# A two-layer transformer on one Trainium2 core: TensorE's order in the expert loop fixed and staggered over three pairs, bank copies on ScalarE

## The chip, the core and the metric

The kernel runs on one core of one Trainium2 chip, in one launch. The time is device microseconds of a whole execution, the lower the better. Three executions of the kernel before took 1410.09, 1410.16 and 1411.47 us; the median is 1410.16 us.

## The reference

The model has two layers over 512 tokens of width 1024, in float32. Layer 0 mixes tokens with differential attention, layer 1 with a compressed, selected and windowed attention; each layer then adds a mixture of 32 experts, of which every token uses two:

```python
pg = softmax(t @ w_grp + b_grp);  p_top, grp = top_k(pg, 1)         # 4 groups of 8 experts
le = einsum('td,gde->tge', t, w_exp) + b_exp                        # router inside a group
val, idx = top_k(le[arange(T), grp[:, 0]], 2)
wts = softmax(val) * p_top
...
a = silu(einsum('td,edh->teh', t, w_gate)) * einsum('td,edh->teh', t, w_up)   # 1024 -> 256, per expert
y = y + einsum('teh,ehd->td', a * combine, w_down)                            # 256 -> 1024
x = x + g2 * y
```

The expert weights of one layer are 32 x 3 MB; all of them pass through the core once per layer.

## The kernel before, in words

After the router, every expert has a list of up to 64 tokens. Two experts make a **pair**: 64 rows of the one and 64 rows of the other fill the 128 partitions. There are 16 pairs a layer, and per pair (function `pair`) these steps:

- **gather** (line 838, a DMA that GpSimd's queue issues): the 128 token rows go to the tile `xg`, which has two buffers.
- **rows** (line 852): 8 transposes of 128x128 on TensorE, four to each of two PSUM banks `tr`; 8 copies out of the banks that apply scale and shift (lines 857 and 859, by turns ScalarE and VectorE) make `xT`.
- **gate-up** (line 864): 16 calls, 8 pieces of the width for each of two experts. Each uses half of the array's columns (64 stationary columns; the output goes to partitions 0 to 63 or 64 to 127), and the two experts' calls run side by side. A call is two MATMUL records in the trace. Then SiLU `sl` on ScalarE (line 867) and the product `ac` on VectorE (line 869).
- **by hidden** (line 873): 2 transposes of `ac` into a `tr` bank and a copy out, `aTm` (lines 394 and 395, by turns ScalarE and VectorE).
- **down** (line 887): 8 calls, again on half of the columns each; then `y` (line 890, VectorE), and its split into two reduced-precision parts, `yh` (line 370, ScalarE) and `yl` (line 371, VectorE).
- **add** (lines 898 and 899): a 0/1 matrix `st` (line 881) scatters the pair's rows back to the tokens: 8 outputs of 128x512 (4 token tiles x 2 halves of the width), each the sum of two matmuls on the full array; VectorE adds each to the residual `xs` (line 900).

Steps on the full 128 stationary columns (rows, by hidden, add) are called **full-tile work** below, gate-up and down **half-column work**. PSUM has 8 banks of 512 floats a partition: four tagged `mm`, two `tr`, two `sc`. A bank is given again when its readers are done. The gate-up's bank and the second half of every down and add are `mm`, the first half of every down and add `sc`.

In the loop of `experts` the add of pair q-1 is called inside pair q, behind its by-hidden transposes. That is the order of the program's text only: the scheduler of the framework orders each engine's instructions itself by a simulated timeline, TensorE's too, so a pair's adds and transposes may be woven into gate-up and down. What an engine does is fixed when the program is built.

Weights come from one queue, that of SyncE (SP, line 114), in pieces of 512 KB. Gate and up of five experts and down of six are in SBUF at a time (`N_GU`, `N_DN`); a piece waits until the matmuls that read its place last are done, and until the piece eight places ahead of it has landed (`DEPTH_X`). Ahead of the loop, `overflow` holds a second copy of the pair's code for experts with more than 64 tokens, behind a branch; with these inputs it isn't entered.

## Time and profile before

| | |
|---|---|
| median of 3 executions | 1410.16 us |
| the profiled execution | 1411.33 us, of which the profile's span 1409.5 us |
| mean granted TensorE clock | 0.956 of full speed |
| TensorE busy | 1282.6 us (91%) |
| VectorE, ScalarE, GpSimd busy | 786.7 us (56%), 514.6 us (37%), 169.4 us (12%) |
| DMA | 309.8 MB, mean 220 GB/s |
| gate-up matmuls (line 864) | 1024 MATMUL records |
| copies out of the `tr` banks (lines 857, 859) | 128 on ScalarE, 128 on VectorE |

The two expert loops lie at about 397 to 679 us (layer 0) and 1117 to 1399 us (layer 1) of the span. The profile's slices show TensorE nearly always busy in them; since matmuls are pipelined and their ends are modelled, that says little, and the loop is better read by the time from pair to pair.

### The profile page before, as it was taken

Reading aid. Unit: us, or ns where it says so; the run is one execution under the profiler, and the core shown is the slowest. Engines: PE = TensorE matmul, PEld = TensorE weight load, DVE = VectorE, ACT = ScalarE, POOL = GpSimd, SP = SyncE. Lnnn points to the kernel's source line nnn. Section 1 sums busy time; section 2 is a strip of 40 time slices with the busy share of each in tenths; the row PEclk is TensorE's granted clock in tenths of the full one; section 3 lists DMA queues with packets and bytes.
Section 4 is the critical chain, followed back from the end, with each engine's and each line's share of the span. In section 5 each row is a group of like instructions: output and inputs, shape, how many; then the busy total and the mean of one; then the engine's idle time right before and its main releaser. Section 6 shows DMA issues by size and latency. Waiting matters only on the chain. (4 is left out here: it accounts for less than half of the span.)

```text
span 1409.5 us, 18225 instructions
## 1 busy us (share of the span) xinstructions
PE 1282.6 (91%) x6431; PEld 759.2 (54%) x6431; DVE 786.7 (56%) x1791; ACT 514.6 (37%) x1188; POOL 169.4 (12%) x298
## 2 busy tenths in 40 slices
PE   4899999978879999999799799999999699999995
PEld 0687668567733544444588555555568434444342
DVE  2454755485635666655554365656635446666555
ACT  2454544454322222111454444656644212222212
POOL 0021020211110000000042111111220200000000
PEclk7899999999989999999899899999999699999998
DMA  7633764585579999992332174510153599999931
GB/s 253 219 104 112 244 209 150 180 289 193 185 244 363 390 405 408 379 350 95 109 120 90 60 255 147 148 51 1 54 161 120 182 362 369 407 408 409 364 141 60
DMA packets 104493, 309.81 MB, mean 220 GB/s; under 512 B 13776, under 2 KB 27568, under 8 KB 104388
## 3 DMA queue, kind: packets, MB, share of 16 engines
q1 hardware_dynamic: 93920, 288.59, 57.4%
q0 software_dynamic: 6240, 12.95, 2.7%
q10 hardware_dynamic: 4228, 6.96, 1.6%
q8 instruction: 55, 0.90, 0.3%
q14 instruction: 50, 0.41, 0.1%
HBM read 310.51 MB, written 6.33 MB: 225 GB/s over the span
## 5 line engine op out<-in xcount | busy, mean ns | idle before, releaser
L864 PE MATMUL b_mm<-slot,xT 128*64 128x512 f32 x640 | 199.3, 604 | 0.0
L864 PE MATMUL b_mm<-ring,xT 128*64 128x512 f32 x384 | 135.9, 597 | 0.0
L362 PE MATMUL b_mm<-wh,h_hi 128*128 128x512 f32 (+1 forms) x320 | 116.1, 394 | 8.3 <-ACT wh L358 6.6
L363 PE MATMUL b_mm<-wl,h_hi 128*128 128x512 f32 (+1 forms) x320 | 122.5, 391 | 0.7 <-DVE wl L359 0.7
L364 PE MATMUL b_mm<-wh,h_lo 128*128 128x512 f32 (+1 forms) x320 | 120.6, 387 | 0.0
L857 ACT ACTIVATE xT<-b_tr,col_sh,col_A 128x128 f32<-128x128 f32 x128 | 56.5, 455 | 148.2 <-DVE xT L859 146.9
L864 PEld LDWEIGHTS b_mm<-slot,xT 128*64 128x64 f32 x640 | 58.1, 139 | 87.3 <-issue 80.6
L900 DVE TENSOR_TENSOR xs<-xs,b_sc 128x512 f32<-128x512 f32 x128 | 83.4, 683 | 23.0 <-PE b_sc L899 23.0
L900 DVE TENSOR_TENSOR xs<-xs,b_mm 128x512 f32<-128x512 f32 x128 | 82.1, 682 | 19.3 <-PE b_mm L899 19.3
L189 PE MATMUL b_mm<-ring,csil 128*32 128x512 f32 x384 | 76.0, 657 | 11.8 <-DMA ring<-in_ada_w_dram 6.9
L838 POOL DMA_INDIRECT xg<-xr_d,toks x32 | 32.0, 1000 | 432.3 <-PE b_tr L852 411.8
L867 ACT ACTIVATE sl<-b_mm 128x256 f32<-128x256 f32 x32 | 12.3, 385 | 186.9 <-PE b_mm L864 186.9
L869 DVE TENSOR_TENSOR ac<-b_mm,sl 128x256 f32<-128x256 f32 x32 | 19.7, 617 | 107.7 <-ACT sl L867 107.7
L359 DVE TENSOR_TENSOR wl<-ring,wh 128x512 fp32r<-128x512 f32 (+1 forms) x80 | 53.1, 672 | 35.9 <-ACT wh L358 34.3
L1216 ACT ACTIVATE pT<-b_tr 128x512 f32<-128x512 f32 x80 | 47.4, 597 | 65.2 <-PE b_tr L1214 64.6
L362 PEld LDWEIGHTS b_mm<-wh,h_hi 128*128 128x128 f32 x320 | 60.3, 191 | 19.9 <-ACT wh L358 7.3
L386 DVE TENSOR_REDUCE nm<-b_sc 128x1 f32<-128x128 f32 (+3 forms) x116 | 54.3, 482 | 27.5 <-PE b_sc L381 26.8
L370 ACT ACTIVATE yh<-y 128x512 fp32r<-128x512 f32 x64 | 39.9, 632 | 79.5 <-DVE y L890 79.5
L363 PEld LDWEIGHTS b_mm<-wl,h_hi 128*128 128x128 f32 x320 | 61.0, 191 | 12.4 <-DVE wl L359 1.4
L358 ACT ACTIVATE wh<-ring 128x512 fp32r<-128x512 f32 (+1 forms) x80 | 48.4, 614 | 50.7 <-PE b_mm L364 36.2
L364 PEld LDWEIGHTS b_mm<-wh,h_lo 128*128 128x128 f32 x320 | 60.8, 190 | 11.1
L864 PEld LDWEIGHTS b_mm<-ring,xT 128*64 128x64 f32 x384 | 39.9, 137 | 49.4 <-issue 46.8
(329 smaller groups left out, 2678.5 us busy)
## 6 DMA issues: line engine op xcount, KB each, us to landing
ring<-in_ada_w_dram SPq DMA_DIRECT2D x96, 512.0 KB, 4.9
slot<-in_moe_w_gate_dram SPq DMA_DIRECT2D x80, 512.0 KB, 8.4
slot<-in_moe_w_up_dram SPq DMA_DIRECT2D x80, 512.0 KB, 4.4
dn<-in_moe_w_down_dram SPq DMA_DIRECT2D x80, 512.0 KB, 8.0
slot<-in_moe_w_down_dram SPq DMA_DIRECT2D x48, 512.0 KB, 8.6
ring<-in_moe_w_gate_dram SPq DMA_DIRECT2D x48, 512.0 KB, 10.1
ring<-in_moe_w_up_dram SPq DMA_DIRECT2D x48, 512.0 KB, 4.4
ring<-in_diff_w_in_dram SPq DMA_DIRECT2D x24, 512.0 KB, 4.8
```

Of the source, the lines that this page charges most:

```text
L189: mm(acc[32 * g:32 * g + 32, :], lhsT, w[:, c0:c0 + 512], start=(k == 0), stop=(k == KC - 1), skip_group_check=True)
L358: nc.scalar.activation(wh[:, :n], w[:, k, :], AF.Copy)
L359: nc.vector.tensor_tensor(wl[:, :n], w[:, k, :], wh[:, :n].bitcast(F32), op=OP.subtract)
L362: mm(accs[t][:, :n], hi[:, k, tt], wh[:, :n], start=(k == 0), stop=False)
L363: mm(accs[t][:, :n], hi[:, k, tt], wl[:, :n], start=False, stop=False)
L364: mm(accs[t][:, :n], lo[:, k, tt], wh[:, :n], start=False, stop=(k == KC - 1))
L370: nc.scalar.activation(h_out, src, AF.Copy)
L386: nc.vector.tensor_reduce(nm, b[:, :n], axis=AX.X, op=OP.max, negate=True)
L857: nc.scalar.activation(xT[:, k, :], src, AF.Identity, scale=g.Ac[:, k:k + 1], bias=g.shc[:, k:k + 1])
L864: mm(hb[64 * a:64 * a + 64, :].rearrange("p (z n) -> p z n", z=2), xT[:, k, 64 * a:64 * a + 64], gu(a, k), start=(k == 0), stop=(k == KC - ...
L900: nc.vector.tensor_tensor(g.xs[:, t, zz], g.xs[:, t, zz], b, op=OP.add)
L1216: nc.scalar.activation(pT, b, AF.Copy)
```

## The change: what it does

`pair` is cut into `rows_in`, `gate_up`, `by_hidden` and `down`, which returns its eight adds as a list. The loop of `experts` calls them in another order:

```diff
+        gather(tab, 1, g.xg[1])
+        pinned.add("PE")
+        xT = rows_in(g, g.xg[0])
+        ac = gate_up(g, xT, gus(0))
+        xT = rows_in(g, g.xg[1])
+        adds = []
         for q in range(NPAIR):
-            e = 2 * q
-            w.fetch(q=q, paced=DEPTH_X)
-            if q:
-                gather(tab, q, g.xg[q % len(g.xg)])
-            add = pair(g, q, tab,
-                       lambda a, k: w.gu(e + a, k), lambda a, k, z: w.dn(e + a, k, z), g.xg[q % len(g.xg)], add)
-        add()
+            nxt = None
+            if q + 2 < NPAIR:
+                gather(tab, q + 2, g.xg[q % 2])
+            w.fetch(q=q + 1, paced=DEPTH_X)
+            if q + 1 < NPAIR:
+                nxt = gate_up(g, xT, gus(q + 1))
+            for a in adds:
+                a()
+            aT = by_hidden(g, ac)
+            if q + 2 < NPAIR:
+                xT = rows_in(g, g.xg[q % 2])
+            adds = down(g, q, tab, aT, lambda a, k, z: w.dn(2 * q + a, k, z))
+            ac = nxt
+        for a in adds:
+            a()
+        pinned.clear()
```

So a turn of the loop is: gate-up of pair q+1; then in one piece the adds of pair q-1, the by-hidden transposes of pair q and the rows of pair q+2; then down of pair q. All matmuls and transposes go through two wrappers, and while `pinned` names TensorE the scheduler must keep them in the order of the text:

```diff
-    mm = nc.tensor.matmul
+    pinned = set()
+    def pin(i, engine):
+        return tc.keep_in_program_order(i) if engine in pinned else i
+    def mm(*a, **k):
+        return pin(nc.tensor.matmul(*a, **k), "PE")
+    def transpose(*a):
+        return pin(nc.tensor.transpose(*a), "PE")
```

The order of the other engines is still the scheduler's. The copies out of the `tr` banks all go to ScalarE:

```diff
-                if kk % 2:
-                    nc.scalar.activation(xT[:, k, :], src, AF.Identity, scale=g.Ac[:, k:k + 1], bias=g.shc[:, k:k + 1])
-                else:
-                    nc.vector.tensor_scalar(xT[:, k, :], src, g.Ac[:, k:k + 1], g.shc[:, k:k + 1],
-                                            op0=OP.mult, op1=OP.add)
+                nc.scalar.activation(xT[:, k, :], b[:, kk * P:(kk + 1) * P], AF.Identity, scale=g.Ac[:, k:k + 1],
+                                     bias=g.shc[:, k:k + 1])
...
-        copy_any(aT.rearrange("p k t -> p (k t)"), b[:, 0:HID])
+        nc.scalar.activation(aT.rearrange("p k t -> p (k t)"), b[:, 0:HID], AF.Copy)
```

The weights' window keeps its size; its bounds are written for the staggered turn, where `fetch` is called with q+1:

```diff
-                if e >= 2 * q + (N_GU if kind == "g" else N_DN):
+                if e >= (2 * q + N_GU if kind == "g" else 2 * max(q - 1, 0) + N_DN):
```

No matmul, transpose or DMA is added or taken away. Outside the two loops and the copy of the pair's code in `overflow`, the built orders agree but for two things: behind each loop the norms of the first token tiles stand among the last additions to `xs`, and one row scaling in layer 1's router stands two instructions later.

The built programs' orders show what moves. (Since the wrappers record every call, matmuls now stand at line 94 and transposes at line 97; a row is known by its tiles.) First TensorE early in layer 0's loop, in the gate-up of the third pair; `slot_` and `ring_` are gate-up weights, `yh` and `yl` belong to adds. Before:

```order
L864 MATMUL b_mm<-slot_6418,xT 64x512
L898 MATMUL b_sc<-yh,st 128x512 x2
L899 MATMUL b_sc<-yl,st 128x512 x2
L864 MATMUL b_mm<-ring_73,xT 64x512
L864 MATMUL b_mm<-slot_6421,xT 64x512
L898 MATMUL b_mm<-yh,st 128x512 x3
L864 MATMUL b_mm<-ring_73,xT 64x512
L864 MATMUL b_mm<-slot_6421,xT 64x512
L899 MATMUL b_mm<-yl,st 128x512
L864 MATMUL b_mm<-ring_73,xT 64x512
L864 MATMUL b_mm<-slot_6421,xT 64x512
L864 MATMUL b_mm<-ring_73,xT 64x512
```

and in the change, at the end of a gate-up:

```order
L94 MATMUL b_mm<-ring_72,xT 64x512
L94 MATMUL b_mm<-ring_73,xT 64x512
L94 MATMUL b_mm<-ring_72,xT 64x512
L94 MATMUL b_mm<-ring_73,xT 64x512
L94 MATMUL b_sc<-yh,st 128x512
L94 MATMUL b_sc<-yl,st 128x512
L94 MATMUL b_mm<-yh,st 128x512
L94 MATMUL b_mm<-yl,st 128x512
L94 MATMUL b_sc<-yh,st 128x512
L94 MATMUL b_sc<-yl,st 128x512
```

Adds that stood in pieces between gate-up calls now stand behind the whole gate-up; the sixteen calls of a pair's adds follow one another, first half (`sc`) and second half (`mm`) of each token tile by turns.

Second, TensorE late in layer 0's loop, from the end of one pair's gate-up; `dn_` and `aTm` are down's operands. Before:

```order
L864 MATMUL b_mm<-ring_73,xT 64x512
L873 MATMUL b_tr<-ident,ac 128x128 x2
L852 MATMUL b_tr<-ident,xg_3359 128x128 x4
L887 MATMUL b_sc<-dn_7732,aTm 64x512
L887 MATMUL b_sc<-dn_7735,aTm 64x512
L887 MATMUL b_sc<-dn_7732,aTm 64x512
L887 MATMUL b_sc<-dn_7735,aTm 64x512
L887 MATMUL b_mm<-dn_7732,aTm 64x512
L887 MATMUL b_mm<-dn_7735,aTm 64x512
L887 MATMUL b_mm<-dn_7732,aTm 64x512
L887 MATMUL b_mm<-dn_7735,aTm 64x512
L852 MATMUL b_tr<-ident,xg_3359 128x128 x4
```

and in the change:

```order
L94 MATMUL b_mm<-yh,st 128x512
L94 MATMUL b_mm<-yl,st 128x512
L97 MATMUL b_tr<-ident,ac 128x128 x2
L97 MATMUL b_tr<-ident,xg_3359 128x128 x8
L94 MATMUL b_sc<-dn_7682,aTm 64x512
L94 MATMUL b_sc<-dn_7685,aTm 64x512
L94 MATMUL b_sc<-dn_7682,aTm 64x512
L94 MATMUL b_sc<-dn_7685,aTm 64x512
L94 MATMUL b_mm<-dn_7682,aTm 64x512
```

Before, the by-hidden transposes stand right behind the gate-up whose product they need, and half of the rows' transposes behind down. Now the adds stand ahead of by hidden, another pair's gate-up stands between a pair's gate-up and its by hidden, and all eight row transposes go with it.

Third, VectorE in the middle of layer 0's loop, one pair. Before:

```order
L890 SCALAR_TENSOR_TENSOR y<-b_sc,tw,bc 128x512
L890 SCALAR_TENSOR_TENSOR y<-b_mm,tw,bc 128x512
L371 TENSOR_TENSOR yl<-y,yh 128x512 x2
L869 TENSOR_TENSOR ac<-b_mm,sl 128x128x2
L900 TENSOR_TENSOR xs<-xs,b_sc 128x512 x2
L900 TENSOR_TENSOR xs<-xs,b_mm 128x512 x4
L859 TENSOR_SCALAR xT<-b_tr,col_A_2994,col_sh_2992 128x128
L900 TENSOR_TENSOR xs<-xs,b_sc 128x512 x2
```

and in the change:

```order
L906 SCALAR_TENSOR_TENSOR y<-b_mm,tw,bc 128x512
L382 TENSOR_TENSOR yl<-y,yh 128x512
L878 TENSOR_TENSOR ac<-b_mm,sl 128x128x2
L914 TENSOR_TENSOR xs<-xs,b_sc 128x512
L914 TENSOR_TENSOR xs<-xs,b_mm 128x512
L914 TENSOR_TENSOR xs<-xs,b_sc 128x512
L914 TENSOR_TENSOR xs<-xs,b_mm 128x512
L914 TENSOR_TENSOR xs<-xs,b_sc 128x512
L914 TENSOR_TENSOR xs<-xs,b_mm 128x512
L914 TENSOR_TENSOR xs<-xs,b_sc 128x512
L914 TENSOR_TENSOR xs<-xs,b_mm 128x512
```

The copies `xT` are gone from VectorE; `ac` stands ahead of all eight additions to `xs`, which go by turns over `sc` and `mm` banks. ScalarE's pair is now `sl`, `aTm`, eight `xT`, two `yh`, in that order, in every turn.

## Rows read from the trace of the kernel before

**Rows 1.** Windows of layer 0's loop; columns: stretch us, length, busy us per engine (instructions), PEclk, DMA share, GB/s.

```profile
455.00:555.00 100.00, 98.97 (x467) 47.69 (x464) 61.31 (x112) 21.60 (x46) 5.91 (x6) 1.00 1.02 399
...
555.00:665.00 110.00, 104.81 (x454) 46.75 (x453) 65.66 (x118) 20.95 (x44) 3.94 (x4) 1.00 0.79 297
```

**Rows 2.** Timeline, ACT, line 867: SiLU after a pair's gate-up; start us, us, ..., idle before, releaser.

```profile
407.23 0.38 ACT L867 ACTIVATE sl<-b_mm 128x256 f32<-128x256 f32 x1 [5.04 <-PE b_mm L864]
...
458.28 0.39 ACT L867 ACTIVATE sl<-b_mm 128x256 f32<-128x256 f32 x1 [4.79 <-PE b_mm L864]
...
553.43 0.39 ACT L867 ACTIVATE sl<-b_mm 128x256 f32<-128x256 f32 x1 [3.95 <-PE b_mm L864]
...
665.59 0.38 ACT L867 ACTIVATE sl<-b_mm 128x256 f32<-128x256 f32 x1 [8.54 <-PE b_mm L864]
...
1127.34 0.38 ACT L867 ACTIVATE sl<-b_mm 128x256 f32<-128x256 f32 x1 [5.14 <-PE b_mm L864]
...
1385.65 0.38 ACT L867 ACTIVATE sl<-b_mm 128x256 f32<-128x256 f32 x1 [8.54 <-PE b_mm L864]
```

**Rows 3.** Timeline, PE, one pair of the steady stretch.

```profile
500.63 0.59 PE L864 MATMUL b_mm<-slot,xT 128*64 128x512 f32 x1
...
505.35 0.59 PE L864 MATMUL b_mm<-slot,xT 128*64 128x512 f32 x1
...
505.88 0.74 PE L898 MATMUL b_sc<-yh,st 128*128 128x512 f32 x2
...
506.45 0.86 PE L898 MATMUL b_mm<-yh,st 128*128 128x512 f32 x3
...
508.32 0.38 PE L873 MATMUL b_tr<-ident,ac 128*128 128x128 f32 x2
...
510.92 1.94 PE L887 MATMUL b_mm<-slot,aTm 128*64 128x512 f32 x8
```

**Rows 4.** Timeline, PE, one early pair (first two rows) and one late pair.

```profile
417.02 0.74 PE L898 MATMUL b_sc<-yh,st 128*128 128x512 f32 x2
...
428.23 3.40 PE L887 MATMUL b_sc<-dn,aTm 128*64 128x512 f32 x8 [2.05 <-DVE aTm L395]
...
611.86 0.44 PE L873 MATMUL b_tr<-ident,ac 128*128 128x128 f32 x2 [1.11 <-DVE ac L869]
...
618.00 0.73 PE L898 MATMUL b_sc<-yh,st 128*128 128x512 f32 x2
```

**Rows 5.** Timeline, DVE and ACT, beside the pair of group 3; then a row of the groups by line.

```profile
506.44 0.63 DVE L869 TENSOR_TENSOR ac<-b_mm,sl 128x256 f32<-128x256 f32 x1 [2.76 <-ACT sl L867]
...
508.74 0.39 ACT L394 ACTIVATE aTm<-b_tr 128x256 f32<-128x256 f32 x1 [2.33 <-PE b_tr L873]
...
508.79 2.47 DVE L900 TENSOR_TENSOR xs<-xs,b_mm 128x512 f32<-128x512 f32 x4
...
L857 ACT ACTIVATE xT<-b_tr,col_sh,col_A 128x128 f32<-128x128 f32 x64 | 28.2, 455 | 72.6 <-DVE xT L859 71.9
```

**Rows 6.** SP's queue waits and DMA issues, 380 to 690 us.

```profile
SPq L114 <- PE b_mm L864: 73.6, 23, 12.2
...
slot<-in_moe_w_down_dram SPq DMA_DIRECT2D x20, 512.0 KB, 8.6
```

**Rows 7.** Timeline, all engines, end of layer 0's loop.

```profile
666.66 0.44 PE L873 MATMUL b_tr<-ident,ac 128*128 128x128 f32 x2 [1.11 <-DVE ac L869]
...
667.61 1.94 PE L887 MATMUL b_sc<-slot,aTm 128*64 128x512 f32 x8 [0.52 <-DVE aTm L395]
...
672.52 0.63 ACT L370 ACTIVATE yh<-y 128x512 fp32r<-128x512 f32 x1 [1.42 <-DVE y L890]
...
675.94 2.48 DVE L900 TENSOR_TENSOR xs<-xs,b_mm 128x512 f32<-128x512 f32 x4
...
680.19 1.06 ACT L326 ACTIVATE junk<-xs 128x1024 bf16<-128x1024 f32 x1
```

More of the change, by code (lines that the diff above doesn't have):

```diff
@@ L469, in x_first @@
             for t in range(NT):
[L470 removed]
+                transpose(b[:, t * P:(t + 1) * P], by_k(o_n[:, t, :])[:, k, :], ident)
             copy_any(xT[k // 4][:, k % 4, :], b)
@@ L546, in diff_rows @@
         for j in range(i + 1):
-            nc.tensor.transpose(b[:, j * P:(j + 1) * P], a[:, j * P:(j + 1) * P], ident)
+            transpose(b[:, j * P:(j + 1) * P], a[:, j * P:(j + 1) * P], ident)
         aT = m.tile([P, 512], F32, name="aT", bufs=2)
@@ L628, in o_trans @@
         for i in range(NT):
-            nc.tensor.transpose(b[:, i * P:(i + 1) * P], o_n[:, i, h * P:(h + 1) * P], ident)
+            transpose(b[:, i * P:(i + 1) * P], o_n[:, i, h * P:(h + 1) * P], ident)
         stack_k(b, o_hi[:, h, :], o_lo[:, h, :])
@@ L840, in gather, with rows_in @@
                                      bounds_check=S - 1, oob_is_err=False)
-    def pair(g, q, tab, gu, dn, xg, between=None):
-        mp = g.mq
-        toks, tokf, wts = tab
+    def rows_in(g, xg):
         xT = g.mp.tile([P, KC, P], F32, name="xT", bufs=2)
@@ L851, in pair, with gate_up @@
                 k = 4 * z + kk
-                nc.tensor.transpose(b[:, kk * P:(kk + 1) * P], by_k(xg)[:, k, :], ident)
+                transpose(b[:, kk * P:(kk + 1) * P], by_k(xg)[:, k, :], ident)
             for kk in range(4):
                 k = 4 * z + kk
-                src = b[:, kk * P:(kk + 1) * P]
-                if kk % 2:
-                    nc.scalar.activation(xT[:, k, :], src, AF.Identity, scale=g.Ac[:, k:k + 1], bias=g.shc[:, k:k + 1])
-                else:
-                    nc.vector.tensor_scalar(xT[:, k, :], src, g.Ac[:, k:k + 1], g.shc[:, k:k + 1],
-                                            op0=OP.mult, op1=OP.add)
+                nc.scalar.activation(xT[:, k, :], b[:, kk * P:(kk + 1) * P], AF.Identity, scale=g.Ac[:, k:k + 1],
+                                     bias=g.shc[:, k:k + 1])
+        return xT
+    def gate_up(g, xT, gu):
+        mp = g.mq
         hb = bank("mm")
@@ L870, in pair, with by_hidden, down @@
                                 sl.rearrange("p (t k) -> p t k", k=2), op=OP.mult)
+        return ac
+    def by_hidden(g, ac):
         b = bank("tr")
         for k in range(2):
-            nc.tensor.transpose(b[:, k * P:(k + 1) * P], ac[:, k * P:(k + 1) * P], ident)
-        aT = mp.tile([P, 2, P], F32, name="aTm", bufs=2)
-        copy_any(aT.rearrange("p k t -> p (k t)"), b[:, 0:HID])
-        if between is not None:
-            between()
+            transpose(b[:, k * P:(k + 1) * P], ac[:, k * P:(k + 1) * P], ident)
+        aT = g.mq.tile([P, 2, P], F32, name="aTm", bufs=2)
+        nc.scalar.activation(aT.rearrange("p k t -> p (k t)"), b[:, 0:HID], AF.Copy)
+        return aT
+    def down(g, q, tab, aT, dn):
+        mp = g.mq
+        toks, tokf, wts = tab
         yh = mp.tile([P, D], F32R, name="yh", bufs=1)
@@ L891, in pair, with add @@
             stack_k(y, yh[:, zz], yl[:, zz])
-        def add():
-            for t in range(NT):
-                for z in range(2):
-                    zz = slice(z * 512, (z + 1) * 512)
-                    b = bank("mm" if z else "sc")
-                    mm(b, st[:, t * P:(t + 1) * P], yh[:, zz], start=True, stop=False)
-                    mm(b, st[:, t * P:(t + 1) * P], yl[:, zz], start=False, stop=True)
-                    nc.vector.tensor_tensor(g.xs[:, t, zz], g.xs[:, t, zz], b, op=OP.add)
-        return add
+        def add(t, z):
+            zz = slice(z * 512, (z + 1) * 512)
+            b = bank("mm" if z else "sc")
+            mm(b, st[:, t * P:(t + 1) * P], yh[:, zz], start=True, stop=False)
+            mm(b, st[:, t * P:(t + 1) * P], yl[:, zz], start=False, stop=True)
+            nc.vector.tensor_tensor(g.xs[:, t, zz], g.xs[:, t, zz], b, op=OP.add)
+        return [lambda t=t, z=z: add(t, z) for t in range(NT) for z in range(2)]
     def experts(l, g, w, later):
@@ L916, in experts, with gus @@
         overflow(l, g, g.xg[-1])
-        add = None
-        for q in range(NPAIR):
-            e = 2 * q
-            w.fetch(q=q, paced=DEPTH_X)
-            if q:
-                gather(tab, q, g.xg[q % len(g.xg)])
-            add = pair(g, q, tab,
-                       lambda a, k: w.gu(e + a, k), lambda a, k, z: w.dn(e + a, k, z), g.xg[q % len(g.xg)], add)
-        add()
+        def gus(q):
+            return lambda a, k: w.gu(2 * q + a, k)
+        gather(tab, 1, g.xg[1])
[4 more added lines that the diff above has]
+        adds = []
+        for q in range(NPAIR):
+            nxt = None
[14 more added lines that the diff above has]
+        pinned.clear()
         g.st2.close()
@@ L957, in overflow @@
                     gather(tab, q, xg)
-                    pair(g, q, tab, gu(q), dn(q), xg)()
+                    for a in down(g, q, tab, by_hidden(g, gate_up(g, rows_in(g, xg), gu(q))), dn(q)):
+                        a()
     g = open_moe(0)
@@ L1082, in tile_kernel @@
     b = bank("tr")
-    nc.tensor.transpose(b[:, 0:32], pos32, ident[0:32, 0:32])
+    transpose(b[:, 0:32], pos32, ident[0:32, 0:32])
     posT = m.tile([P, 32], F32, name="posT")
@@ L1128, in tile_kernel @@
     for k in range(2):
-        nc.tensor.transpose(b[:, k * P:(k + 1) * P], hc[:, k * P:(k + 1) * P], ident)
+        transpose(b[:, k * P:(k + 1) * P], hc[:, k * P:(k + 1) * P], ident)
     hcT = m.tile([P, 2, P], F32, name="hcT", tag="pcT", bufs=2)
```

19 lines of the change are left out of this document (9 added, 10 removed).

## The prediction

> **What bounds the kernel now.** I read the windows of the expert loop first, then the time from pair to pair, then TensorE's timeline inside single pairs, then the queue waits. In the windows the reader is to see two stretches of one loop: from 455 to 555 us the DMA engines are full (share 1.02, 399 GB/s), from 555 to 665 us they are not (0.79, 297 GB/s), while TensorE counts as busy in both and its granted clock is 1.00 [rows 1]. So busy time doesn't tell which limits. The SiLU of a pair comes when its gate-up ends, so its starts mark the pairs. Layer 0 [rows 2]: 407.23 to 458.28 us is 3 intervals, 51.05 us, 17.0 each; to 553.43 us 6 intervals, 95.15 us, 15.86 each; to 665.59 us 6 intervals, 112.16 us, 18.69 each. Together 258.36 us; layer 1 has 258.31 us. The loop is thus slow at its start and over its last six pairs, and the last six are slow though the DMA has room: over the loop SP's queue waits 73.6 us for gate-up matmuls to free buffers [rows 6], and the list of waits has no matmul of the loop waiting for a weight DMA. What bounds these stretches is TensorE's own order.
>
> What the order costs shows in three rows. Early, adds begin at 417.02 us in the midst of a gate-up; its `aTm` is then copied on VectorE behind a queue of additions, and down starts after 2.05 us of idleness, its first eight records taking 3.40 us instead of 1.94 [rows 3, 4]. Late, by hidden stands right behind its own gate-up and waits 1.11 us for `ac`, and the adds, at 618.00 us, split the next gate-up [rows 4].
>
> **The change, step by step.** I build the new pair interval from the steady pair's rows.
>
> Gate-up: 11 steps of two side-by-side records from 500.63 to 505.35 us, 0.43 us each; 16 make 6.88 us. Down: 8 such steps, 3.44 us. All full-tile work of a pair, 16 add matmuls and 10 transposes with the change of shape on both sides, goes from 505.88 to 510.92 us: 5.04 us; there the adds cost 0.234 us each (eight from 506.45 to 508.32) [rows 3]. Sum 15.36 us: what a pair needs on TensorE with no wait. The waits that the new order adds, neither of which this trace contains:
>
> - *Adds against VectorE.* `ac` now stands ahead of the additions on VectorE. It starts 0.56 us after the adds do and takes 0.63 us [rows 3, 5], so the first addition starts at +1.2 us and each takes 0.62 us (2.47 for four). The seventh add output reuses the `sc` bank of the third, free at 1.2 + 3 x 0.62 + 0.1 = 3.2 us; TensorE would reach it at 0.1 + 6 x 0.467 = 2.9 us. Wait 0.3 us. Bounds: nothing (`ac` later than the first additions) and 0.9 us (two banks late).
> - *Transposes against ScalarE.* By hidden and rows now take three `tr` banks in a row, and there are two: the second four transposes wait until `aTm` is copied. That copy starts 0.42 us after the transposes (508.32 to 508.74) and takes 0.39 us [rows 3, 5], so they start at about 0.9 instead of 0.5 us. Wait 0.4 us; bounds nothing and 0.5.
>
> 15.36 + 0.3 + 0.4 is 16.06 us; but adds and transposes no longer alternate, and of the 5.04 us, 1.30 are not adds (16 x 0.234 = 3.74); I put 0.2 of them to the alternation. I take **15.9 us**, between 15.36 and 16.3.
>
> Gone is by hidden's wait for `ac`: a whole gate-up and the adds of another pair stand between. Nor will adds wait for `yh` and `yl`: 6.88 us of gate-up stand between down and its adds, and the chain `y`, `yh`, `yl` twice takes 6.2 us from the first matmul of down, 3.44 us earlier (667.61 to 673.15, and 0.69 for `yl`) [rows 7].
>
> Copies on ScalarE: 8 x 0.455 = 3.64 us a pair where 4 x 0.455 = 1.82 stood [rows 5]. I cost them at nothing. They start with the transposes, and the gate-up that needs them begins a whole down (3.44 us) later and takes one copy per 0.86 us. Should that cover go, the price is up to 1.82 us a pair. ScalarE then has 8 copies, `aTm`, two `yh` and `sl`, 5.7 of 15.9 us; VectorE loses 1.6 us. The trace speaks for it: ScalarE's 64 copies of layer 0 waited 71.9 us for VectorE's copies from the same bank [rows 5]; the two engines took turns, not halves. The Trainium skill (TensorEngine Tiling (Array Packing), PSUM Bottleneck) advises the opposite: use both ScalarE and VectorE to empty PSUM. By that rule the sum would rise by those 1.82 us a pair; in the order here down hides them.
>
> Weights: the window is the same, but down of a pair now ends two gate-ups later, so its buffers come free later, and in SP's order the pieces behind wait too. A pair moves 12 pieces of 512 KB; the loop has run six pairs at 15.86 us with the DMA full [rows 1, 2], so 15.9 us can be fed. Behind two down experts (4 pieces, some 5 us at the full rate) come the next pair's gate and up, needed a pair later; 8.6 us from issue to landing [rows 6] leaves about 5 us. I cost it at nothing, with the DMA-bound rival below. The gathers are issued two pairs ahead.
>
> Now the sum of one layer, from the first gate-up's end. Second gate-up's end: 8 transposes and the first copy, 1.3 us, and 6.88, so 8.2 us. Third: transposes 1.5, down 3.44, gate-up 6.88, 11.8 us. Then 13 intervals of 15.9, 206.7. Together 226.7 us against 258.36: **-31.7 us**; by stretches, the first three intervals give 35.9 for 51.05, the middle six 95.4 for 95.15, the last six 95.4 for 112.16. The end gets longer: before, from the last gate-up (665.5) to the last down 2.1 us (667.61) and to the fourth norm's square 15.7 us (ends at 681.25) [rows 7]. Now the adds of pair 14 (4.1) and by hidden (0.95, 666.66 to 667.61) come first, then down's start to the last addition: VectorE is free of `y` and `yl` at +6.25 and makes eight additions of 0.62, so +11.3 instead of +10.8 us (675.94 + 2.48); the squares of the first tiles run beside the additions, since these now finish tile by tile, and only the last (1.06) follows. 4.1 + 0.95 + 11.3 + 1.2 = 17.6 us, +1.9. So -29.8 us a layer, **-59.6 us** for both.
>
> Against the profiled execution, 1411.3 us, that gives 1351.7; the median of the runs is 1.2 us lower, so I predict **1351 us**. The bounds of the pair interval, 15.36 and 16.3, over 26 intervals are -14 and +10 us: 1337 to 1361.
>
> **The rivals.**
>
> *The DMA binds.* The middle stretch ran at the full rate before, and the new order frees down's buffers later. If the queue runs dry for 1 to 2 us a pair, the interval is 16.9 to 17.9 us and the time 1351 + 26 x 1.0 to 2.0 = 1377 to 1403 us; with half a microsecond, 1364. For it: share 1.02. Against it: six pairs at 15.86 us without a wait for weights. 13%.
>
> *The copies decide.* The Trainium skill's advice names the case. ScalarE copies eight banks' quarters alone; if gate-up waited for all of them, 1.82 us over 28 pairs, +51 us: 1402 us. Against it: 3.44 us of down stand between. 2%.
>
> *Slower than before.* A fixed order can't work around a late operand. When the first weight of a gate-up is late, all that follows stands still, where the old order had other work woven in. Were the two down experts' pieces and the half expert behind them to land later than one pair after down's end, every pair would wait. The interval must rise over 18.2 us (26 x 2.3 = 59.6) for the change to lose; at 19 us it is 1351 + 26 x 3.1 = 1432 us. Rows for it: SP's 73.6 us of waits for gate-up matmuls [rows 6]. Against it: the 5 us left above would have to turn into minus 2.3. 3%.
>
> *It doesn't do what it says.* The built order shows the pieces moved, so only a time-neutral result is left: the three stretches would have to be bounded by the DMA after all, which the room in the last six pairs contradicts [rows 1]. 1410 us, 2%.
>
> *Better than forecast*, both waits absent and the start tighter: under 1337 us, 4%.
>
> **How the numbers follow.** Forecast (interval 15.36 to 16.3) 76%, DMA 13%, copies 2%, slower 3%, neutral 2%, better 4%. The predicted time is the forecast's, 1351 us. The range for 8 in 10 takes the forecast's bounds, 1337 to 1361, and of the DMA case the part up to half a microsecond a pair and a little over: 1337 to 1368 us. A measurement of this kernel can tell about 0.2%, 2.8 us, from no change. Faster: 76 + 13 + 2 + 4 = 95%; same 2%; slower 3%.
>
> **What would show it.** SiLU starts 15.4 to 16.3 us apart from the fourth to the last, in both layers, with the second 8 us after the first; no adds between gate-up records; by hidden without a wait for `ac`; small waits of transposes for `aTm` and of the seventh add for an addition to `xs`; about 256 copies of 0.455 us on ScalarE and none on VectorE; a DMA share near 1.0 until shortly before the loop's end. It would be wrong if gate-up matmuls waited for weight DMAs pair after pair, if intervals grew along the loop, or if the intervals fell to 15.9 us and the span didn't.

## The result, and the profile after

The changed kernel takes **1377.24 us** (median of 4 runs, 1375.50 to 1377.73) against 1410.82 us for the kernel before on the same chip (4 runs, 1410.09 to 1413.0). The ratio is 0.9747, with a 95% interval of 0.9731 to 0.9763. The forecast was 1351 us and its range 1337 to 1368 us: the direction was right, the gain is 33.6 us and not 59.6, and the time lies outside the range. The profiled execution took 1377.56 us, of which the span is 1375.5 us.

The SiLU starts mark the ends of the gate-ups, as in [rows 2]. In the timeline of ScalarE (start us, us, engine, line, operation and tiles, idle before and releaser), now at line 876:

```profile
409.17 0.38 ACT L876 ACTIVATE sl<-b_mm 128x256 f32<-128x256 f32 x1 [5.67 <-PE b_mm L94]
417.57 0.38 ACT L876 ACTIVATE sl<-b_mm 128x256 f32<-128x256 f32 x1 [4.85 <-issue]
429.62 0.38 ACT L876 ACTIVATE sl<-b_mm 128x256 f32<-128x256 f32 x1 [5.20 <-PE b_mm L94]
...
636.45 0.39 ACT L876 ACTIVATE sl<-b_mm 128x256 f32<-128x256 f32 x1 [5.05 <-PE b_mm L94]
...
1111.83 0.38 ACT L876 ACTIVATE sl<-b_mm 128x256 f32<-128x256 f32 x1 [6.15 <-PE b_mm L94]
...
1339.32 0.39 ACT L876 ACTIVATE sl<-b_mm 128x256 f32<-128x256 f32 x1 [5.05 <-PE b_mm L94]
```

The second SiLU comes 8.4 us after the first and the third 12.05 us later (forecast 8.2 and 11.8); from 429.62 to 636.45 us there are 13 intervals, 206.83 us, **15.91 us each** (forecast 15.9). First to last SiLU is 227.28 us (227.49 in layer 1) for 258.36 [rows 2], forecast 226.7. So the loop's body is what was forecast, and what is missing from the gain went elsewhere. One pair in TensorE's timeline, answering to [rows 3]:

```profile
524.91 0.50 PE L94 MATMUL b_sc<-yh,st 128*128 128x512 f32 x1
...
527.83 0.50 PE L94 MATMUL b_sc<-yh,st 128*128 128x512 f32 x1
...
528.87 0.38 PE L97 MATMUL b_tr<-ident,ac 128*128 128x128 f32 x2
529.08 1.35 PE L97 MATMUL b_tr<-ident,xg 128*128 128x128 f32 x8
530.36 1.94 PE L94 MATMUL b_sc<-dn,aTm 128*64 128x512 f32 x8
...
533.84 7.04 PE L94 MATMUL b_mm<-ring,xT 128*64 128x512 f32 x32
```

Adds, by hidden, rows, down, gate-up, each in one piece. The eight rows take 1.35 us where such transposes without a wait take 1.05 (a run below shows it), which is the wait for `aTm`; the seventh add (527.83 us) comes hardly late, 0.1 us and not 0.3. From 430 to 636 us the list of TensorE's waits is empty; in the kernel before it had by hidden for `ac` and down for `aTm`, as in [rows 4]. Waits are not all that went: in the late pair of [rows 4], one expert's first gate-up call stands alone ahead of the adds (617.00 us, 1.0 us), the rest takes 7.08 us from 621.92 us on, so gate-up takes 8.1 us there and 7.0 here, where the two experts run side by side throughout. The windows, answering to [rows 1] (stretch, length, busy us and instructions per engine, granted clock, DMA share, GB/s):

```profile
455.00:555.00 100.00, 99.81 (x468) 46.50 (x466) 52.51 (x87) 30.22 (x73) 5.94 (x6) 1.00 1.02 399
555.00:625.00 70.00, 69.87 (x328) 35.85 (x324) 38.11 (x63) 20.29 (x50) 2.97 (x3) 1.00 1.03 408
```

The DMA engines are full to 625 us. The share of 0.79 from 555 to 665 us in [rows 1] reads like room over all of the last six pairs of the kernel before, and the prediction read it so; but it is the mean of two stretches, as narrower windows of that kernel show:

```profile
595.00:630.00 35.00, 32.86 (x142) 14.12 (x138) 19.72 (x35) 7.05 (x15) 1.97 (x2) 1.00 0.97 360
630.00:665.00 35.00, 33.67 (x148) 15.00 (x148) 19.67 (x36) 6.74 (x14) 0.00 (x0) 1.00 0.36 123
```

To 630 us the share was near 1 there too, at 360 GB/s (392 from 560 to 595 us) for 408 now; only over the last two pairs did the DMA engines stand mostly idle. ScalarE makes all 256 copies of `xT` (467 ns each, 455 in [rows 5]). SP's queue waits 69.2 us for matmuls into `mm` banks, a row that doesn't tell gate-up from the second half of down, over the stretch where it waited 73.6 us for gate-up [rows 6] and another 74.3 for down. Its waits for earlier pieces of the expert weights to land rose to 113.9 us from 50.2: the transfers themselves now hold it more than the buffers do.

What took the rest back stands behind the last SiLU. The timeline at the end of layer 0's loop, TensorE and (ACT) the square of the fourth norm on ScalarE, answering to [rows 7]:

```profile
636.34 0.50 PE L94 MATMUL b_sc<-yh,st 128*128 128x512 f32 x1
...
640.30 0.38 PE L97 MATMUL b_tr<-ident,ac 128*128 128x128 f32 x2
...
646.72 0.49 PE L94 MATMUL b_mm<-yh,st 128*128 128x512 f32 x1 [0.82 <-ACT yh L381]
...
650.57 0.38 PE L97 MATMUL b_tr<-ident,ac 128*128 128x128 f32 x2
...
660.64 0.40 PE L94 MATMUL b_mm<-yl,st 128*128 128x512 f32 x1
...
662.71 1.06 ACT L337 ACTIVATE junk<-xs 128x1024 bf16<-128x1024 f32 x1
...
663.39 0.55 PE L97 MATMUL b_tr<-ident,slot 128*128 128x128 f32 x2 [2.35 <-DVE r_h L338]
```

After the gate-up of pair 15 (it ends at 636.4 us) TensorE still has the adds of pair 13, by hidden and down of pair 14, the adds of pair 14, and only at 650.57 us by hidden, down and adds of pair 15. From the last SiLU to the end of the fourth square are 27.3 us (636.45 to 663.77; layer 1: 1339.32 to 1366.62) for 15.7 us before. The balance of the profiled executions:

| stretch | before | after | change | forecast |
|---|---|---|---|---|
| layer 0, first rows' transposes to first SiLU | 10.2 us | 12.3 us | +2.2 | 0 |
| layer 0, first to last SiLU | 258.4 | 227.3 | -31.1 | -31.7 |
| layer 0, last SiLU to fourth square's end | 15.7 | 27.3 | +11.7 | +1.9 |
| layer 1, the same three | 10.3, 258.3, 15.7 | 12.8, 227.5, 27.3 | +2.5, -30.8, +11.6 | 0, -31.7, +1.9 |
| sum | | | -33.9 | -59.6 |
| the span | 1409.5 | 1375.5 | -34.0 | |

The three stretches carry the whole difference of the spans. The start is the smaller loss. ScalarE and TensorE at the first pair of layer 0, then two windows, and two of the kernel before:

```profile
398.01 1.28 ACT L863 ACT_TABLE_LOAD   x1 [9.39 <-PE b_tr L97]
...
399.82 9.31 PE L94 MATMUL b_mm<-slot,xT 128*64 128x512 f32 x32 [1.02 <-ACT xT L863]
```

```profile
400.00:402.00 2.00, 2.00 (x6) 0.80 (x7) 0.00 (x0) 2.00 (x7) 0.21 (x1) 0.50 0.76 236
402.00:404.30 2.30, 2.30 (x8) 0.78 (x6) 0.00 (x0) 1.49 (x2) 0.00 (x0) 0.51 0.14 48
```

```profile
399.00:401.40 2.40, 2.40 (x7) 0.71 (x8) 1.14 (x3) 1.92 (x5) 1.13 (x2) 0.53 0.51 132
401.40:403.00 1.60, 1.60 (x10) 0.56 (x8) 0.00 (x0) 0.79 (x1) 0.00 (x0) 1.00 0.56 177
```

In the kernel before, VectorE made the first copy, and ScalarE's table was loaded before the rows came (394.32 us). Now the first copy is ScalarE's and stands behind a table load of 1.28 us, so the gate-up starts 3.0 us after the transposes where it was 1.9. It then runs at a granted clock of 0.50 (the 1.2 GHz level) to 404.3 us, where before the clock was up from 401.4 us on; gate-up takes 9.31 us for 8.21. The Trainium skill (ScalarE activation tables: per-element evaluation and per-set limits, What a function is on this engine) gives 1283 ns for the table load between two functions of different sets; the trace agrees, 1.28 us.

### The profile page after: what moved, and what is told of

It reads as the page before. It is cut to its first block, busy times and chain, and to the rows that moved or that the text cites. A ratio compares the mean times of both kernels' runs of the same rounds, so it can differ in the third digit from the quotient of the medians.

```text
span 1375.5 us, 18124 instructions
## 1 busy us (share of the span) xinstructions
PE 1264.3 (92%) x6431; PEld 765.6 (56%) x6431; DVE 733.4 (53%) x1647; ACT 558.2 (41%) x1332; POOL 171.9 (12%) x298
## 4 chain that ended last, share of the span: by engine, by line
PE 45%; DVE 2%; ACT 2%; DMA 1%; issue 1%; POOL 0%; ACTq 0%; POOLq 0%; DVEq 0%
PE b_mm L94 31%; PE b_sc L94 8%; PE b_tr L97 6%; DMA xg<-xr_d,toks 1%; DMA xr_d<-xr 0%; DVE nm L397 0%; DVE xs L914 0%; DVE y L906 0%; DVE yl L382 0%; ACT yh L381 0%; DVE slot L1242 0%; ACTq L1117 0%; POOL rs L179 0%; DVE otmp L618 0%; DVE blk L1137 0%
## 5 line engine op out<-in xcount | busy, mean ns | idle before, releaser
L94 PE MATMUL b_mm<-slot,xT 128*64 128x512 f32 x640 | 188.3, 609 | 2.2 <-ACT xT L863 2.0
L94 PE MATMUL b_mm<-ring,xT 128*64 128x512 f32 x384 | 126.9, 592 | 0.0
L94 PEld LDWEIGHTS b_mm<-slot,xT 128*64 128x64 f32 x640 | 62.7, 141 | 91.3 <-issue 78.2
L863 ACT ACTIVATE xT<-b_tr,col_sh,col_A 128x128 f32<-128x128 f32 x256 | 92.8, 467 | 2.5 <-PE b_tr L97 0.5
L914 DVE TENSOR_TENSOR xs<-xs,b_mm 128x512 f32<-128x512 f32 x128 | 86.8, 678 | 2.4 <-PE b_mm L94 2.4
L914 DVE TENSOR_TENSOR xs<-xs,b_sc 128x512 f32<-128x512 f32 x128 | 87.0, 679 | 0.0
L876 ACT ACTIVATE sl<-b_mm 128x256 f32<-128x256 f32 x32 | 12.3, 384 | 163.7 <-PE b_mm L94 153.9
L94 PE MATMUL b_sc<-slot,slot 128*128 128x128 f32 (+3 forms) x232 | 71.8, 384 | 5.7 <-ACT es L398 3.1
L94 PEld LDWEIGHTS b_mm<-ring,xT 128*64 128x64 f32 x384 | 43.8, 137 | 50.7 <-issue 47.4
L369 ACT ACTIVATE wh<-ring 128x512 fp32r<-128x512 f32 (+1 forms) x80 | 48.4, 614 | 50.2 <-PE b_mm L94 36.4
L94 PEld LDWEIGHTS b_mm<-wl,h_hi 128*128 128x128 f32 x320 | 61.1, 192 | 12.3 <-DVE wl L370 1.4
```

Source lines behind the costliest of these rows:

```text
L94: return pin(nc.tensor.matmul(*a, **k), "PE")
L369: nc.scalar.activation(wh[:, :n], w[:, k, :], AF.Copy)
L863: nc.scalar.activation(xT[:, k, :], b[:, kk * P:(kk + 1) * P], AF.Identity, scale=g.Ac[:, k:k + 1], bias=g.shc[:, k:k + 1])
L876: nc.scalar.activation(sl, hb[:, 0:HID], AF.Silu)
L914: nc.vector.tensor_tensor(g.xs[:, t, zz], g.xs[:, t, zz], b, op=OP.add)
```

## The experiments

The theory after the result (A): a pair costs one interval wherever it stands, so a gate-up that the stagger (a gate-up one pair ahead of its by hidden) pulls forward at the start is paid for behind the last SiLU, and the loop is worth 16 intervals. 16 x 15.9 is 254.4 us; from the first SiLU to the fourth square's end are 254.6 us in layer 0 (254.8 in layer 1) against 274.0 before. The rivals: B, the next phase starts late for reasons of its own; C, the copies on ScalarE took the missing time; D, the stagger brings the gain; E, fixing the order does nothing.

**1. The last gate-up put late.**

```diff
-            if q + 1 < NPAIR:
+            if q + 2 < NPAIR:
                 nxt = gate_up(g, xT, gus(q + 1))
...
             adds = down(g, q, tab, aT, lambda a, k, z: w.dn(2 * q + a, k, z))
+            if q + 2 == NPAIR:
+                nxt = gate_up(g, xT, gus(q + 1))
```

> The changed kernel, but in the last turns the gate-up of pair 15 runs behind the down projection of pair 14 instead of ahead of the additions of pair 13. Theory A (the missing time is the drain: each of the 16 pairs costs 15.9 us wherever it stands, so a gate-up that the stagger pulled forward is paid for behind the last SiLU): the last SiLU starts about 24 us after the one before it instead of 15.9 us, the stretch from the last SiLU to the next phase's first transposes shrinks from 26.9 us to about 19 us, and the sum of both stays, so the time stays at 1377 us within 2 us. Rival B (the next phase itself starts late, for its own weights or queues): the stretch behind the last SiLU stays near 27 us, and with the SiLU 8 us later in each of two layers the time is about 1393 us.

It took 1381.51 us (1378.48 to 1383.87; ratio 0.9787, 0.9767 to 0.9807). ScalarE's and then TensorE's timeline of this run:

```profile
621.26 0.38 ACT L876 ACTIVATE sl<-b_mm 128x256 f32<-128x256 f32 x1 [5.08 <-PE b_mm L94]
...
647.46 0.38 ACT L876 ACTIVATE sl<-b_mm 128x256 f32<-128x256 f32 x1 [5.03 <-PE b_mm L94]
```

```profile
661.34 0.39 PE L94 MATMUL b_mm<-yl,st 128*128 128x512 f32 x1
664.10 0.49 PE L97 MATMUL b_tr<-ident,slot 128*128 128x128 f32 x2 [2.37 <-DVE r_h L338]
```

The last SiLU comes 26.2 us after the one before it, and the stretch from it to the next phase's transposes shrinks to 16.6 us from 26.9 (636.45 to 663.39): the gate-up was moved by 10.3 us and the stretch behind it lost 10.3. From the first SiLU (409.93) to the last add's end are 251.8 us, in the changed kernel 251.9 (409.17 to 661.04). B falls: it wanted 27 us and 1393 us. The time is 4 us above the changed kernel's, outside the 2 us I had allowed, while the profiled span is only 0.9 us longer (1376.4); that remainder is not explained.

**2. No stagger: fixed order over two pairs.**

```diff
-        ac = gate_up(g, xT, gus(0))
-        xT = rows_in(g, g.xg[1])
...
+            ac = gate_up(g, xT, gus(q))
             for a in adds:
                 a()
             aT = by_hidden(g, ac)
-            if q + 2 < NPAIR:
-                xT = rows_in(g, g.xg[q % 2])
+            if q + 1 < NPAIR:
+                xT = rows_in(g, g.xg[(q + 1) % 2])
             adds = down(g, q, tab, aT, lambda a, k, z: w.dn(2 * q + a, k, z))
-            ac = nxt
```

The weights' window has its old bounds, and the gathers go one pair ahead.

> The changed kernel with the order still fixed and the copies still on ScalarE, but without the stagger: in a turn gate-up, additions of the pair before, by hidden, rows of the next pair, down, all of this pair but the additions. Theory A: the steady interval between SiLUs stays at 15.9 us, the loop still costs 16 of them; at the end one chain y to yl is uncovered instead of two (1.4 us back) and one wait for aTm (0.5), at the start SiLU and ac of pair 0 are uncovered (1.1 us), so 1376 us within 3 us. Rival D (the stagger is what brings the gain): the interval goes back to about 17.2 us and the time to about 1410 us.

It took 1376.64 us (ratio 0.9742, 0.9720 to 0.9764): the same as the changed kernel. ScalarE's timeline:

```profile
410.15 0.38 ACT L876 ACTIVATE sl<-b_mm 128x256 f32<-128x256 f32 x1 [5.68 <-PE b_mm L94]
423.37 0.39 ACT L876 ACTIVATE sl<-b_mm 128x256 f32<-128x256 f32 x1 [5.07 <-PE b_mm L94]
...
646.36 0.38 ACT L876 ACTIVATE sl<-b_mm 128x256 f32<-128x256 f32 x1 [5.03 <-PE b_mm L94]
```

The second SiLU comes 13.2 us after the first (8.4 with the stagger), then 14 intervals of 15.93 us. The first SiLU to the last is 236.2 us, 8.9 more than with the stagger, and from the last SiLU to the last add's end it is 8.7 us less (15.9 for 24.6). D falls: the stagger is worth nothing here. Eight additions of the pair before are cover enough for SiLU and `ac`.

**3. All copies shared again, and 4. only the `xT` copies shared.**

```diff
-                nc.scalar.activation(xT[:, k, :], b[:, kk * P:(kk + 1) * P], AF.Identity, scale=g.Ac[:, k:k + 1],
-                                     bias=g.shc[:, k:k + 1])
+                src = b[:, kk * P:(kk + 1) * P]
+                if kk % 2:
+                    nc.scalar.activation(xT[:, k, :], src, AF.Identity, scale=g.Ac[:, k:k + 1], bias=g.shc[:, k:k + 1])
+                else:
+                    nc.vector.tensor_scalar(xT[:, k, :], src, g.Ac[:, k:k + 1], g.shc[:, k:k + 1],
+                                            op0=OP.mult, op1=OP.add)
...
-        nc.scalar.activation(aT.rearrange("p k t -> p (k t)"), b[:, 0:HID], AF.Copy)
+        copy_any(aT.rearrange("p k t -> p (k t)"), b[:, 0:HID])
```

Run 4 has the first part of this alone.

> The changed kernel with the xT and aTm copies shared between VectorE and ScalarE as in the kernel before. Theory A (the copies on ScalarE cost nothing and are part of the gain): VectorE's half of the copies stands behind the additions, which leave VectorE only about 1.7 us after by hidden, so xT comes 0.5 to 1.6 us late and the interval is 16.4 to 17.5 us: 1393 to 1428 us, most likely 1405 us. Rival C (the missing 26 us went into the eight ScalarE copies in a row): the interval falls below 15.9 us, to about 15.1 us, and the time to about 1351 us.

> The changed kernel with the xT copies shared between VectorE and ScalarE again and the aTm copy left on ScalarE. Theory A2 (in the run with all copies shared only every second pair was long, the one whose aTm copy stood behind the eight additions on VectorE): no wait for aTm, all intervals 15.9 to 16.1 us, and as the first xT copy is VectorE's again, the first SiLU of each layer comes about 2 us earlier: 1372 to 1380 us, most likely 1374 us. Rival (it is the xT copies behind the additions that were late): intervals stay at 17 us or more, 1405 to 1415 us.

With all copies shared: 1414.97 us (ratio 1.0025, 1.0011 to 1.0040), nothing of the gain is left. With the `xT` copies alone shared: 1376.77 us (0.9748, 0.9725 to 0.9771), all of it is there. In the first of the two, every second SiLU interval is 15.9 us, and the seven between them are 17.7 us four times and 19.4 us three times, in both layers (478.82, 494.72, 514.10, 530.00, 547.74 us: 15.9, 19.4, 15.9, 17.7). Two long ones in TensorE's timeline, and a window of the first:

```profile
501.25 0.80 PE L97 MATMUL b_tr<-ident,xg 128*128 128x128 f32 x4 [1.85 <-DVE aTm L406]
...
501.97 3.49 PE L94 MATMUL b_sc<-dn,aTm 128*64 128x512 f32 x8
...
536.53 0.71 PE L97 MATMUL b_tr<-ident,xg 128*128 128x128 f32 x4 [1.85 <-DVE aTm L406]
537.17 1.94 PE L94 MATMUL b_sc<-dn,aTm 128*64 128x512 f32 x8
```

```profile
502.00:504.70 2.70, 2.70 (x9) 0.85 (x10) 1.14 (x3) 1.26 (x3) 0.99 (x1) 0.50 1.01 393
```

In every second pair the `aTm` copy is VectorE's, behind eight additions (at 500.77 us in the first of these two); the second four transposes of rows, which need its bank, wait 1.85 us: an interval of 17.7 us. In three of the seven, TensorE's granted clock is then at 0.50 for 2.7 us, and down's first eight records take 3.49 us for 1.94, another 1.55 us: 19.4. The kernel before had the same pair of costs in [rows 4] (2.05 us idle, then 3.40 for 1.94). C falls, and the part of the change that matters among the copies is one a pair, `aTm`, not the eight of `xT`. My expectation for run 3 had the time right (1393 to 1428 us) and the place wrong: I had the `xT` copies late.

**5. The order not fixed**, the line `pinned.add("PE")` taken out.

> The changed kernel without the fixed order of TensorE: the same staggered text, and the scheduler sets the order. Theory A (fixed order and ScalarE copies together make the interval of 15.9 us): additions slip between gate-up matmuls again, interval 16.2 to 17 us, time 1385 to 1412 us, most likely 1395 us. Rival E (fixing the order does nothing, the text's order and the copies do it): 1377 us within 3 us.

It took 1414.29 us (ratio 1.0022, 1.0010 to 1.0034), above the range of either theory. TensorE's timeline in one pair:

```profile
521.47 1.35 PE L97 MATMUL b_tr<-ident,xg 128*128 128x128 f32 x8
523.84 0.73 PE L94 MATMUL b_sc<-yh,st 128*128 128x512 f32 x2 [1.02 <-ACT yh L381]
...
525.23 3.65 PE L94 MATMUL b_mm<-slot,xT 128*64 128x512 f32 x16
528.81 0.95 PE L94 MATMUL b_mm<-yh,st 128*128 128x512 f32 x3
```

Left free, the scheduler puts adds right behind rows, where they wait 1.02 us for a `yh` that is not made yet, and more adds into the middle of the gate-up (525.23, 528.81 us). From the fourth SiLU on the intervals scatter between 15.3 and 22.9 us (24.4 in layer 1). The staggered text and the copies without the fixed order are worth nothing; rival E falls.

**6. The kernel before with all copies on ScalarE, and 7. the kernel before with its own text's order fixed.** Run 6 has the diff of the copies as in the change. Run 7 adds the wrappers and, around the loop,

```diff
         add = None
+        pinned.add("PE")
         for q in range(NPAIR):
...
         add()
+        pinned.clear()
```

> The kernel before, with all xT and aTm copies on ScalarE and nothing else changed. Theory A (the gain needs the fixed order and an aTm copy that VectorE's additions cannot hold up, both together): the scheduler's order stays as loose as before, the mean interval between SiLUs stays near 17.2 us, time 1405 to 1416 us, most likely 1411 us. Rival (the copies alone carry it): interval 15.9 us, time about 1377 us.

> The kernel before with nothing changed but that TensorE's order in the expert loop is fixed as its text has it (rows, gate-up, by hidden, additions of the pair before, down; copies shared as before). Theory P (fixing an order is worth only what that order covers): SiLU and ac (1.1 us) and the first xT copies (about 1 us) lie open in each pair, interval 17.3 to 18.5 us, time 1412 to 1450 us, most likely 1430 us. Rival (that the scheduler's mixing of narrow and full tiles is what costs, so any fixed order gains): under 1400 us.

Run 6 took 1425.46 us (ratio 1.0093, 1.0072 to 1.0113), slower than expected; run 7 took 1420.17 us (1.0067, 1.0041 to 1.0093), near its expectation. TensorE's two longest waits from 430 to 640 us, of run 6 and then of run 7 (what waited for what: us in total, times, longest):

```profile
PE b_tr L869 <- DVE ac L865: 4.9, 5, 1.1
PE b_mm L894 <- DVE xs L896: 2.5, 3, 0.8
```

```profile
PE b_tr L96 <- DVE ac L879: 13.3, 12, 1.1
PE b_mm L93 <- DVE xT L869: 4.9, 11, 0.5
```

In run 6 the first seven pairs run 14.6 to 15.8 us apart (first to eighth SiLU, 409.59 to 517.20 us), the last eight 18.3 to 20.9 us: the scheduler puts by hidden right behind its own gate-up again. The waits for `ac` and `xs` explain only part of that: from 520 to 673 us they are 9.3 us, while the eight long intervals lie together some 33 us above eight at the mean of the first seven. As before, gate-up is split there (one expert's first call alone at 581.61 us). In run 7 the pairs are 17.57 us apart from the second on, with 1.1 us for `ac` and about 0.45 us for the first `xT` copy in each. So the parts by themselves make the kernel 0.2 to 0.9% slower than the kernel before, and of what was tried only a fixed order, one whose steps cover each other, together with an `aTm` copy that no queue of additions holds up, gives the 2.5%. The order of run 7 with `aTm` on ScalarE was not tried; its 1.1 us for `ac` in each pair doesn't hang on that copy.

**8. The start: the first pair's copies shared.**

```diff
-        xT = rows_in(g, g.xg[0])
+        xT = rows_in(g, g.xg[0], share=True)
```

With `share`, every other copy of that call is VectorE's, the first one among them.

> The changed kernel, but the xT copies of a layer's first pair alone are shared between VectorE and ScalarE, so that the first one does not wait for ScalarE's table load. Theory S (the 1.9 to 2.5 us lost ahead of the first SiLU are the table load of 1.28 us in front of the first copy, and the half clock that TensorE keeps that much longer): transposes of the first rows to the first SiLU 10.3 us instead of 12.8 us, in both layers, time 1372 to 1374 us. Rival (they come from the gathers or from what stands ahead): no change, 1377 us.

The profiled span fell to 1372.4 us from 1375.5, and the time is 1375.98 us (1374.16 to 1380.19; ratio 0.9755, 0.9735 to 0.9774), which the interval doesn't tell from the changed kernel's. The first pair of layer 1, all engines, with its SiLU:

```profile
1096.71 1.28 ACT L868 ACT_TABLE_LOAD   x1 [4.85 <-ACTq L988]
1098.83 1.95 PE L97 MATMUL b_tr<-ident,xg 128*128 128x128 f32 x8 [3.69 <-DVEq L988]
...
1109.05 0.39 ACT L880 ACTIVATE sl<-b_mm 128x256 f32<-128x256 f32 x1 [5.09 <-PE b_mm L94]
```

The table is loaded before the rows arrive, and transposes to SiLU take 10.2 us for 12.8: theory S holds in the stretch that it speaks of (layer 0: 10.3 for 12.3). Of these 4.6 us the span gives back 3.1; in the time, 3 us are within the scatter of these runs.

**9. By hidden behind four of the eight additions.**

```diff
-            for a in adds:
+            for a in adds[:4]:
                 a()
             aT = by_hidden(g, ac)
+            for a in adds[4:]:
+                a()
```

> The changed kernel, but by hidden of a pair is put behind the first four of the eight additions instead of behind all of them. Theory T (the rows' transposes wait some 0.2 us a pair for a bank that the aTm copy still reads, and in the last two pairs down waits 0.47 us for aTm): 30 x 0.2 + 4 x 0.47 = 8 us less if both go and nothing new appears, interval 15.7 us, time 1369 to 1374 us. Rival (the bank is not what sets the 15.9 us): interval 15.9 us, time 1375 to 1377 us.

It took 1370.07 us (ratio 0.9711, 0.9689 to 0.9733). TensorE's rows, then a window, then TensorE at the start of a later gate-up:

```profile
525.29 1.05 PE L97 MATMUL b_tr<-ident,xg 128*128 128x128 f32 x8
```

```profile
552.00:617.00 65.00, 65.00 (x299) 36.38 (x298) 34.08 (x56) 19.94 (x49) 2.97 (x3) 1.00 1.03 408
```

```profile
576.57 1.02 PE L94 MATMUL b_mm<-ring,xT 128*64 128x512 f32 x2
577.24 0.61 PE L94 MATMUL b_mm<-slot,xT 128*64 128x512 f32 x1
```

The rows take 1.05 us, the wait is gone, and from 443.88 to 552.33 us seven intervals are 15.49 us each. Then four take 64.49 us, 16.1 each: the DMA engines are at 1.03 and 408 GB/s, and the expert whose weights are in `slot` starts 0.67 us after the one in `ring`. The list of waits names no weight here, but the first `up` piece of that expert was issued at 566.89 us, and pieces in this stretch took 10.2 to 11.0 us to land. A pair moves 12 pieces of 512 KB and a gather of 0.27 MB, 6.56 MB together; at 408 GB/s that is an estimated 16.1 us, just what these four take. The pairs at 15.49 us, and those at 15.9 us in the changed kernel, thus drew on pieces that lay ready. This is the DMA-bound rival of the prediction, and it shows once the pairs run below the interval that I forecast. My expectation had the time right (1369 to 1374 us) partly by luck: the interval fell by 0.4 us and not 0.2, and the weights took part of that back.

**10 and 11. The three edits together, staggered and not.** Run 9's edit, run 8's edit, and the last additions ordered by half:

```diff
-        for a in adds:
+        for a in adds[0::2] + adds[1::2]:
             a()
         pinned.clear()
```

Run 10 has them on the changed kernel, run 11 on the kernel of run 2.

> The changed kernel with three edits: by hidden behind the first four additions (this alone measured 1370.1 us), the first pair's xT copies of a layer shared with VectorE (this alone brought the span from 1375.5 to 1372.4 us), and the last eight additions ordered by half, so that the first four do not wait for the second half's yh and yl. If they add up: 1370.1 - 3.1 - 2 x 0.5 = 1366 us, 1363 to 1369 us; if the weights' transfers have become the bound in the later half of the loop, the first-pair edit only moves the wait and it stays at 1369 to 1371 us.

> The same three edits on the order without the stagger (gate-up, four additions of the pair before, by hidden, the other four, rows of the next, down). Theory A: the same as the staggered version or up to 2 us less, as the loop's end leaves one chain from y to yl uncovered instead of two: 1363 to 1369 us. Rival (the stagger hides late weights of the down projections): 3 us or more above the staggered one.

Staggered 1367.80 us (ratio 0.9697, 0.9670 to 0.9723), as expected; without the stagger **1359.64 us** (0.9637, 0.9615 to 0.9659), better than either theory had it and the best kernel of the study. ScalarE's SiLU in run 11, and TensorE's waits from 430 to 640 us in run 10:

```profile
420.00 0.39 ACT L880 ACTIVATE sl<-b_mm 128x256 f32<-128x256 f32 x1 [5.06 <-PE b_mm L94]
...
636.78 0.39 ACT L880 ACTIVATE sl<-b_mm 128x256 f32<-128x256 f32 x1 [5.02 <-PE b_mm L94]
```

```profile
PE b_mm L94 <- DMA slot<-in_moe_w_up_dram: 0.4, 2, 0.2
```

Without the stagger all 14 intervals are 15.48 us, to the last, and the list of TensorE's waits is empty; with it, the later ones are 16 us and more (551.24 to 616.68 us is 65.44 us for four), and matmuls wait for weights. From the first SiLU to the last add's end are 242.7 us against 247.7. I had put this rival the wrong way round: the stagger doesn't hide late weights, it asks for the gate-up's weights a pair sooner out of buffers of the same number. SP's queue speaks for it: from 430 to 640 us it waits 24.8 us for matmuls to free places in run 10 and 11.9 us in run 11. But whether the gate-up's buffers hold it or the down pieces ahead of them, as the prediction had it, was not told apart, and neither was tried with more buffers.

## Why the prediction missed

- **The interval was right**, its terms less so. 15.91 us measured, 15.9 forecast. Of the two waits in it, that of the transposes for `aTm` is real (0.3 us of run 9's 0.4 us gain a pair; forecast 0.4), that of the seventh add is 0.1 us for 0.3. The 0.2 us taken off for the alternation don't show: without its waits the full-tile work takes 5.05 us (5.04 before). Gate-up and down take 0.1 us more than counted. That the sum comes to a tenth is luck; the mechanism is the one described. First to last SiLU: 227.3 and 227.5 us for 226.7.
- **The copies cost nothing in the body, as forecast**; the copies rival is out (runs 3 and 4). Sharing the `xT` copies as the Trainium skill (TensorEngine Tiling (Array Packing), PSUM Bottleneck) advises gives the same time here, 1376.8 us, so it neither helps nor hurts in this order; sharing `aTm` too costs 38 us. The kernel before with ScalarE alone for all copies is 13 us slower (run 6), which is the direction of that advice; but the scheduler then builds another order, so what the copies themselves cost there isn't shown.
- **The step that failed is the term "the end gets longer", +1.9 us a layer.** It said that "the adds of pair 14 (4.1) and by hidden (0.95, 666.66 to 667.61) come first", then down. But over three pairs the last gate-up is followed by the adds of pair 13 and by a whole by hidden, down and adds of pair 14. By hidden of pair 15 stands at +14.1 us from the last SiLU and not at +4.1; from there on the working held (13.2 us to the fourth square's end, 13.5 forecast). With no gate-up left between down and its adds, the adds of pairs 14 and 15 also wait 1.2 us each for `yh` and `yl`, which the prediction had ruled out. Measured +11.7 and +11.6 us: 9.7 us a layer, 19.5 of the 25.7 us between the two sums of the balance. Runs 1 and 2 show it as a move and not as a loss: with the gate-up put late, or without the stagger, SiLUs and the stretch behind them shift by 9 to 10 us and the sum stays.
- **The start was left out**: +2.2 and +2.5 us, a table load that the first copy now waits for and the lower clock behind it (run 8), 4.7 us. The rest, 1.5 us, is the body's 0.6 and 0.9 us.
- **The DMA rival** hardly shows at 15.9 us: near the loop's end one interval of layer 0 and two of layer 1 are 16.0 to 16.1 us. It binds below that (runs 9 and 10), so the lower bound of the interval, 15.36, did not hold to the end in the staggered order. That six pairs at 15.86 us had run with the DMA full didn't show that 15.9 us can be fed for good: by the estimate in run 9 a pair needs 16.1 us, and the pieces that lay ready carried the rest.
- **"Slower" and "it doesn't do what it says"** are out: the list of waits names no weight for a matmul of the loop, and the order is kept. The prediction's own sign of being wrong, intervals at 15.9 us and a span that doesn't follow, is what came.

A shorter sum would have caught it: a loop of 16 pairs that TensorE bounds takes 16 intervals and one uncovered chain (the last pair's steps that no other pair's work covers), however it is staggered. 16 x 15.9 = 254.4 us against the 274.0 us from the first SiLU of the kernel before to its fourth square is -19.6 us a layer, 1372 us in all; with the start's 4.7 us it is 1377. This counts one gate-up too many (7.0 us, ahead of the first SiLU) and leaves out the chain (some 7.2 us, known only from the trace after); that the two cancel is luck.

## What to carry to other kernels

Price a re-staggered loop from its first work to its last, as the number of turns times the interval plus what stays uncovered at the end, and never by the distance of one marker: work pulled ahead of the marker at the start stands behind it at the end. When an order is fixed, look for the one small copy on the path whose engine has a queue ahead of it; here a 0.4 us copy in every second pair decided over the whole gain. And try the same fixed order without the stagger, since a stagger needs its inputs earlier from the same buffers.
